# One start address modulo 256 for all pages and slots of a decoder layer on one core

## The chip, the core and the metric

The kernel runs on one core of a Trainium2 chip. A core has TensorE (PE, matrix multiplication), VectorE (DVE), ScalarE (ACT), GpSimd (POOL), and SyncE (SP), which here only issues DMAs. A matmul is two instructions: a load of the weights (the stationary operand, 128 x 128 here) and the MATMUL that streams the moving operand, up to 512 columns, from the on-chip memory SBUF and adds into PSUM. The metric is the device time of one execution in microseconds (us); lower is better.

## The reference

One hybrid decoder layer in fp32 over 1,040 positions (16 meta tokens and 1,024 tokens) of width 1,024:

```python
h = h + 0.5 * rms_norm(swiglu(rms_norm(h, g_ffn1_pre), w_ffn1_in, w_ffn1_out), g_ffn1_post)
u = rms_norm(h, g_mix_pre)
q, k, v, f_logit, c_b, c_c, c_in, gate_a, gate_c = split_cols(u @ w_in)
y_attn = forgetting_attention(q, k, v, log_sigmoid(f_logit + b_forget)) @ w_attn_branch
y_conv = (c_b * short_conv(c_c * c_in, conv_w)) @ w_conv_branch
mixed = (sigmoid(gate_a) * y_attn + sigmoid(gate_c) * y_conv) @ w_out
h = h + rms_norm(mixed, g_mix_post)
h = h + 0.5 * rms_norm(swiglu(rms_norm(h, g_ffn2_pre), w_ffn2_in, w_ffn2_out), g_ffn2_post)
```

The feed-forward width is 2,816 (22 tiles of 128), there are 8 heads of 64, and the meta positions are dropped at the end.

## The kernel before, in words

**Split products.** Each fp32 operand is split into a rounded part h (type fp32r) and a rest l; a product is three matmuls, h·h, h·l and l·h (`mm3`, lines 137 to 141). `split_into` makes the parts: ScalarE casts (L134), VectorE subtracts (L135).

**Seven products.** The feed-forward blocks and their output products each use a scheme of seven half-size products (P1 to P7) in place of eight. In `ffn_in` there are 22 tiles t; each loads its weights on SyncE, splits them into pages, and runs P1, P2, P6, P7, P5, P4, P3. In the first block (names `w...`) the operands of P1, P2, P6 and P4 have rows of W0 = 528 elements and are streamed as two halves of 264 columns; P7, P5 and P3 stream 512. In the second block (names `v...`) all stream 512: 7 products of 12 matmuls. The results go to DRAM (g1d, g2d).

**Output products.** `product_out` (first block, psum names P1 to P7) and `product2` (second block, names 2P1 to 2P7) read g1d or g2d and w_out back, batch by batch of two k tiles; `prep_a` makes the weights side (ahP, alP), `prep_b` the moving side (bhP, blP). For the next products sums are kept in the running buffers RA and RB. `mix_input` normalises the result and makes the mixer's input um0 (meta tokens and the first 512 tokens) and um1 (the last 512), again as h and l, with 4 k tiles in a slot. V's weights wv come right behind, as two pairs: 264 columns wide (half 0, with the forget logits) and 256 wide (half 1).

**Memory.** Four pools stand one behind the other in SBUF. `const` is small and unchanged. `rg` has pages by use: 4 for h, 4 for l, 3 for raw loads r, each of 1,056 elements (4,224 bytes). `zp` has 14 slots z00 to z13 of 2,112 elements (8,448 bytes) for operands of a whole stage. `lp` has ten pages L0 to L9 of 1,056 elements. A page is given again when all that read it is done. In the built program the eight h and l pages begin at 64 and 192 modulo 256 by turns, and so do the pages of `lp`; every slot begins at 192. A row of 528 elements is 2,112 bytes, 64 more than a multiple of 256.

**What sets the order.** A scheduler puts each engine's instructions in one fixed order when the kernel is built, from a timeline that it plans itself and from the priorities in the code (`tc.high_priority` for loads and splits). At run time an engine works off its list and waits where an operand isn't ready; what stands behind waits too. ScalarE also issues DMAs. A change of buffers changes dependencies, and so that order. The first two b tiles of P1 (k0 = 0 and 2, `early`) take pages of `rg`, because they are split while the last tile of the block still runs.

Of the kernel before, what the change touches and what calls it, by code (L numbers as in the profile page):

```python
# [8 lines left out]
F32 = mybir.dt.float32  # L9
F32R = mybir.dt.float32r  # L10
# [3 lines left out]
P = 128  # L14
D = 1024
KT = D // P
META = 16
SEQ = 1024
L = SEQ + META
# [10 lines left out]

H = 512
W0 = H + META


CQ, CK, CV, CCB, CCC, CCI, CGA = 0, 512, 1024, 1544, 2056, 2568, 3080
# [28 lines left out]
def hybrid_layer(ctx, tc, x, meta, w_in, b_forget, conv_w, w_attn, w_conv, w_out,  # L64
# [8 lines left out]
    V, S, G = nc.vector, nc.scalar, nc.gpsimd  # L73
# [10 lines left out]
    pp = ctx.enter_context(tc.tile_pool(name="pp", bufs=1, space=PSUM, reuse_waits="tile"))  # L84

    def page(tag, n, name):
        return rg.tile([P, 1056], F32 if tag == "r" else F32R, tag=tag, bufs=3 if tag == "r" else 4, name=name)[:, :n]

    def slot(i, a, name, dt=F32R):

# [3 lines left out]
    def blk4(i, n, name, dt=F32R):  # L94
        return zp.tile([P, 4 * W0], dt, tag=f"z{i:02d}", name=name)[:, :4 * n].rearrange("p (k n) -> p k n", k=4)

# [3 lines left out]
    class Turns:  # L100
# [8 lines left out]

        def page(self, name, dt=F32):  # L110
            i = self.turn()
            return lp.tile([P, 2 * W0], dt, tag=f"L{i}", name=name)

        def bank(self, name):
            i = self.turn()
# [17 lines left out]
    def split_into(h, l, src, eng=None):  # L133
        S.copy(h, src)  # L134
        (eng or V).tensor_sub(l, src, f32(h))  # L135
# [324 lines left out]

    U, C11, C21, Vt = (blk4(i, W0, nm, F32) for i, nm in ((1, "y01"), (0, "y00"), (2, "y10"), (3, "y11")))

    def running(slots, n, nm):
        ts = [blk4(i, n, f"{nm}{i}", F32) for i in slots]
# [1 line left out]

    runA, runB = running((7, 8, 9), H, "RA"), running((4, 5, 6), W0, "RB")

    def tileA(tag, k, name):
        return page(tag, k * H, name).rearrange("p (k c) -> p k c", k=k)

    def tileB(tag, k, c, name, early=False):
        t = page(tag, k * c, name) if early else loc[tag].page(name, F32 if tag == "r" else F32R)[:, :k * c]
        return t.rearrange("p (k c) -> p k c", k=k)

    def a_src(f, kh, k0, nk):
# [27 lines left out]
    def prep_b(pr, k0, nk):  # L506
        nm = f"{pr}_{k0}"
        c = H if pr in ("P7", "P5", "P3") else W0
        r = slice(META, W0)
        early = pr == "P1" and k0 < 4  # L510
        with tc.high_priority():
            B = lambda kh, hh: b_src(kh, hh, k0, nk)
            tb = lambda tag, n, x: tileB(tag, nk, n, f"b{x}{nm}", early)
            if pr == "P5":
                R = tb("r", H, "r")
                load(R, B(0, 1))
                t = tb("r", W0, "r2")
                load(t, B(0, 0))
                V.tensor_sub(R, R, t[:, :, r])
                h, l = tb("h", c, "h"), tb("l", c, "l")  # L520
                split_into(h, l, R)
                return Split(h, l)
            R = runB(k0, nk)
            if pr == "P7":
                load(R[:, :, r], B(0, 1))
            raw = tb("r", c, "r")
            load(raw, B(*{"P1": (0, 0), "P2": (1, 0), "P3": (1, 1), "P7": (1, 1), "P6": (0, 0), "P4": (1, 0)}[pr]))
            h, l = tb("h", c, "h"), tb("l", c, "l")
            if pr in ("P1", "P2", "P3"):
                split_into(h, l, raw)  # L530
            elif pr == "P7":
                V.tensor_sub(R[:, :, r], raw, R[:, :, r])
                split_into(h, l, R[:, :, r])
            elif pr == "P6":
                V.tensor_add(R[:, :, r], raw[:, :, r], R[:, :, r])
                V.tensor_copy(R[:, :, :META], raw[:, :, :META])
                split_into(h, l, R)
            else:
                V.tensor_sub(R, raw, R)
                split_into(h, l, R)  # L540
        return Split(h, l)
# [3 lines left out]
    def drain(pr, ms, ps):  # L545

        with tc.high_priority():
            if len(ms) == 1:
                m = ms[0]
                for q, p in enumerate(ps):  # L550
                    w = W0 // 2
                    src = p[:, :w]
                    vw = lambda t: t[:, m, q * w:q * w + w]
                    if pr == "P1":
                        S.copy(vw(U), src)
                    elif pr == "P2":
                        V.tensor_add(vw(C11), vw(U), src)
                    elif pr == "P6":
                        V.tensor_add(vw(Vt), vw(Vt), src)
                        V.tensor_add(vw(U), vw(U), src)  # L560
                    else:
                        V.tensor_add(vw(C21), vw(Vt), src)
            else:
                for m, p in zip(ms, ps):
                    vw = lambda t: t[:, m, rr]
                    if pr == "P7":
                        G.tensor_copy(Vt[:, m, :META], U[:, m, :META])
                        V.tensor_add(vw(Vt), vw(U), p)
                    elif pr == "P5":
                        V.tensor_add(vw(Vt), vw(Vt), p)  # L570
                        V.tensor_add(vw(U), vw(U), p)
                    else:
                        V.tensor_add(vw(U), vw(U), p)
# [4 lines left out]
    def product_out(pr, ps=None):  # L578
        ps = ps or banks_out(pr)
        if pr in ("P7", "P5", "P3"):  # L580
            for k0, nk in batches(2):
                a, b = prep_a(pr, k0, nk), prep_b(pr, k0, nk)
                for k in range(nk):
                    for m in range(4):
                        mm3(ps[m // 2][m % 2], a.at(ALLP, k, slice(m * P, m * P + P)), b.at(ALLP, k),
                            start=k0 + k == 0, stop=k0 + k == FH - 1)
            for j in range(2):
                drain(pr, (2 * j, 2 * j + 1), ps[j])
        else:
            w = W0 // 2  # L590
            for k0, nk in batches(2):
                a, b = prep_a(pr, k0, nk), prep_b(pr, k0, nk)
                for k in range(nk):
                    for m in range(4):
                        for q in range(2):
                            mm3(ps[m][q][:, :w], a.at(ALLP, k, slice(m * P, m * P + P)),
                                b.at(ALLP, k, slice(q * w, q * w + w)), start=k0 + k == 0, stop=k0 + k == FH - 1)
            for m in range(4):
                drain(pr, (m,), ps[m])
# [4 lines left out]
    def mix_input(half):  # L604

        if half == 0:
            g = pages2(11, "g1p")
            gain_row(g[:, 0], g1_post, half=True)
            gain_row(g[:, 1], gm_pre)
            grow[0] = g  # L610
        g = grow[0]
        ys = ((C11, C21), (U, Vt))[half]
        hs, ls = ((4, 5), (6, 10)) if half == 0 else ((7, 8), (9, 0))
        h, l = ([blk4(i, W0, f"um{half}{x}{f}") for f, i in enumerate(t)] for x, t in (("h", hs), ("l", ls)))
        um_[half] = (h, l)

        def enter(i):
            o, wd = BLK[i][1], P if i else META
            py = [psR(f"yp{i}_{f}")[:wd] for f in range(2)]
            for f in range(2):  # L620
                for k in range(4):
                    nc.tensor.transpose(py[f][:, k * P:(k + 1) * P], ys[f][:, k, o:o + wd], ident)
            if half == 0:
                w = pages2(12 + i % 2, f"w1_{i}")
                w = [w[:, 0], w[:, 1]]
            else:
                w = [loc[t].page(f"w1{t}{i}")[:, :D] for t in "rh"]
            rows_ = x[(i - 1) * P:i * P, :] if i else meta
            token_block(py, rows_, h1d[(i - 1) * P:i * P, :] if i else None, g[:, 0], w, wd, f"m{i}")
            return w  # L630

        def leave(i, w):
            o, wd = BLK[i][1], P if i else META
            pts = token_cols(g[:, 1], w, psR, wd, f"m{i}")
            for f in range(2):
                split_into(h[f][:, :, o:o + wd], l[f][:, :, o:o + wd], pts[f])

        staggered([i for i in range(9) if BLK[i][0] == half], enter, leave)

    for pr in ("P1", "P2", "P7", "P6", "P4"):  # L640
        product_out(pr)
    psQ, psR = Turns(0, 1, 2, 3).bank2, Turns(4, 5, 6, 7).bank
    ps = banks_out("P5")
    mix_input(0)
# [12 lines left out]
        return t.rearrange("p a n -> p (a n)")[:, :shape[0] * shape[1]].rearrange("p (a n) -> p a n", a=shape[0])  # L657

    wv = {}
    for half, (c0, w) in enumerate(VHALF):  # L660
        for q in range(2):
            src = w_in[512 * q:512 * q + 512, c0:c0 + w].rearrange("(k p) c -> p k c", p=P)
            wv[half, q] = unit([(src, 0)], f"wv{half}_{q}", kt=4, w=w)
    z = const.tile([P, 9, NH], F32, name="z")

    def um(half, k, c0, n):
        h, l = um_[half]
        return Split(h[k // 4][:, k % 4, c0:c0 + n], l[k // 4][:, k % 4, c0:c0 + n])

    def values_in(blk, pvs):  # L670
# [507 lines left out]
```

## Time and profile before

| | us |
|---|---|
| median of 3 runs | 2278.13 (2277.70 to 2285.56) |
| the profiled execution | 2279.55 |
| its span, first to last instruction | 2277.6 |
| TensorE busy | 2150.1 |
| VectorE busy | 1435.8 |
| ScalarE busy | 775.6 |

The mean granted clock of TensorE over the span is 0.974 (1 is 2.4 GHz, 0.5 is 1.2 GHz). Successive matmuls overlap in the pipeline: the duration of one is not its pace. The pace is read from the start of one matmul to the start of the next in the timeline.

### The profile page before, as it was taken

How to read it: one execution, taken by the hardware profiler on the slowest of the kernel's cores; microseconds unless marked ns; L12 is line 12 of the kernel's file. 1: busy time of each engine (PE TensorE's matmuls, PEld its weight loads, DVE VectorE, ACT ScalarE, POOL GpSimd, SP SyncE). 2: the span in 40 equal slices, each digit the busy share in tenths (PEclk: the TensorE clock that was granted, in tenths of full speed). 3: DMA queues.
4: the chain of work that ended last, by engine and by line, in shares of the span. 5: the costliest groups of instructions: out<-in, count | busy, mean ns of one | idle time of the engine just before them, and what ended most of it. 6: DMA issues, size and time to landing. Idle time of an engine off the chain costs nothing.

```text
span 2277.6 us, 30019 instructions
## 1 busy us (share of the span) xinstructions
PE 2150.1 (94%) x11622; PEld 1849.7 (81%) x11622; DVE 1435.8 (63%) x2332; ACT 775.6 (34%) x1269; POOL 100.9 (4%) x194
## 2 busy tenths in 40 slices
PE   5899999999998999999999999899799999999995
PEld 5799999989886998888878787787688888878874
DVE  7866666645969643345554447756776666647785
ACT  5322222223334421134343435334322222224332
POOL 1000000000001100000000001010000000000000
PEclk9899999999998999999999999999899999999998
DMA  3322222266657542343433283843232222278672
GB/s 131 102 84 84 84 84 71 84 243 209 194 164 231 165 145 69 97 115 94 130 105 107 62 229 119 265 138 102 64 112 83 75 78 78 77 261 269 194 263 102
DMA packets 275462, 305.44 MB, mean 134 GB/s; under 512 B 12812, under 2 KB 181848, under 8 KB 275320
## 3 DMA queue, kind: packets, MB, share of 16 engines
q1 hardware_dynamic: 239568, 242.94, 35.4%
q10 hardware_dynamic: 35720, 60.59, 7.7%
q8 instruction: 91, 1.49, 0.3%
q14 instruction: 51, 0.42, 0.1%
q0 software_dynamic: 32, 0.00, 0.0%
HBM read 233.47 MB, written 57.36 MB: 128 GB/s over the span
## 4 chain that ended last, share of the span: by engine, by line
PE 82%; DMA 8%; DVE 6%; issue 2%; ACT 2%; SPq 0%; POOL 0%; ACTq 0%; DVEq 0%; POOLq 0%
PE wP L139 6%; PE wP L140 6%; PE wP L141 6%; PE vP L141 6%; PE vP L140 6%; PE vP L139 6%; PE 2P L140 2%; PE 2P L141 2%; PE 2P L139 2%; PE pg L139 2%; PE pg L141 2%; PE pg L140 2%; PE P L140 2%; PE P L141 2%; PE P L139 2%
## 5 line engine op out<-in xcount | busy, mean ns | idle before, releaser
L139 PE MATMUL P<-bhP,ahP 128*128 128x264 f32 (+1 forms) x484 | 147.8, 323 | 14.5 <-ACT bhP L134 10.3
L140 PE MATMUL P<-blP,ahP 128*128 128x264 f32 (+1 forms) x484 | 157.2, 326 | 4.0 <-DVE ms_m0b L181 3.7
L141 PE MATMUL P<-bhP,alP 128*128 128x264 f32 (+1 forms) x484 | 156.2, 325 | 0.7 <-DVE alP L135 0.7
L140 PE MATMUL 2P<-lb2P,ha2P 128*128 128x512 f32 x308 | 122.5, 398 | 6.1 <-DVE lb2P L135 6.1
L141 PE MATMUL 2P<-hb2P,la2P 128*128 128x512 f32 x308 | 121.8, 396 | 0.0
L139 PE MATMUL 2P<-hb2P,ha2P 128*128 128x512 f32 x308 | 113.7, 396 | 3.8 <-ACT hb2P L134 2.3
L139 PEld LDWEIGHTS P<-bhP,ahP 128*128 128x128 f32 x484 | 91.6, 193 | 22.5 <-ACT bhP L134 11.7
L140 PEld LDWEIGHTS P<-blP,ahP 128*128 128x128 f32 x484 | 95.3, 197 | 11.2 <-DVE ms_m0b L181 4.1
L141 PEld LDWEIGHTS P<-bhP,alP 128*128 128x128 f32 x484 | 95.1, 197 | 7.2 <-DVE alP L135 1.0
L135 DVE TENSOR_TENSOR hbc<-tp,hbc 128x512 fp32r<-128x512 f32 (+1 forms) x112 | 67.2, 610 | 24.3 <-ACT hbc L134 23.5
L134 ACT CAST hbc<-tp 128x512 fp32r<-128x512 f32 (+1 forms) x112 | 56.8, 525 | 62.1 <-PE tp L905 54.8
L140 PEld LDWEIGHTS 2P<-lb2P,ha2P 128*128 128x128 f32 x308 | 58.7, 191 | 20.6 <-DVE lb2P L135 7.4
L139 PEld LDWEIGHTS 2P<-hb2P,ha2P 128*128 128x128 f32 x308 | 57.9, 189 | 18.4 <-ACT hb2P L134 3.5
L141 PEld LDWEIGHTS 2P<-hb2P,la2P 128*128 128x128 f32 x308 | 58.6, 191 | 13.3 <-DVE la2P L135 0.3
L879 PE MATMUL sc<-k,q 128*128 128x392 f32 (+6 forms) x224 | 56.5, 347 | 6.0 <-DMA k<-ha 2.5
L884 ACT ACTIVATE p<-p,mn 128x1040 f32<-128x1040 f32 (+3 forms) x64 | 50.5, 790 | 31.2 <-DVE mn L880 27.3
L139 PE MATMUL wP<-u1T4h,w 128*128 128x264 f32 x176 | 51.4, 292 | 4.5 <-ACT w L134 4.5
L139 PE MATMUL pg<-um0h,g_h 128*128 128x512 f32 x128 | 50.9, 398 | 2.1 <-ACT gt L806 2.1
L139 PE MATMUL pg<-um1h,g_h 128*128 128x512 f32 x128 | 51.6, 403 | 1.2 <-ACT gt L806 0.8
L139 PE MATMUL wP<-u1T2h,ws32h 128*128 128x264 f32 x176 | 50.6, 289 | 1.1 <-ACT u1T2h L134 1.1
L140 PE MATMUL wP<-u1T2l,ws32h 128*128 128x264 f32 x176 | 50.8, 289 | 0.8 <-DVE u1T2l L135 0.8
L141 PE MATMUL pg<-um1h,g_l 128*128 128x512 f32 x128 | 51.1, 400 | 0.0
(769 smaller groups left out, 6720.5 us busy)
## 6 DMA issues: line engine op xcount, KB each, us to landing
arP<-in_w_ffn_out_dram SPq DMA_DIRECT2D x35, 512.0 KB
ra2P<-g2d SPq DMA_DIRECT2D x35, 512.0 KB
rb2P<-in_w_ffn_out_dram SPq DMA_DIRECT2D x35, 512.0 KB
wrb<-in_w_ffn_in_dram SPq DMA_DIRECT2D x22, 512.0 KB
vrb<-in_w_ffn_in_dram SPq DMA_DIRECT2D x22, 512.0 KB
g2d<-vuc ACTq DMA_DIRECT2D x44, 256.0 KB
brP<-g1d SPq DMA_DIRECT2D x20, 528.0 KB
wra<-in_w_ffn_in_dram SPq DMA_DIRECT2D x19, 512.0 KB
```

Of the source, the lines that this page charges most:

```text
L134: S.copy(h, src)
L135: (eng or V).tensor_sub(l, src, f32(h))
L139: mm(o, a.h, b.h, start=start, stop=False)
L140: mm(o, a.h, b.l, start=False, stop=False)
L141: mm(o, a.l, b.h, start=False, stop=stop)
L879: mm(sc[:, :ke - k0], q[:, s, qt * P:qt * P + P], k[:, k0:ke], start=s == 0, stop=s == 1)
L884: S.activation(p[:, :nk], p[:, :nk], AF.Exp, bias=low, scale=-1.0, accum_out=mn[:, 3:4])
```

## The change

Pages and slots get lengths that are multiples of 256 bytes: h and l pages 1,024 elements, r pages and the pages of `lp` 1,088; slots had one already. With that all of them begin at 64 modulo 256. What no longer fits into 1,024 elements moves: the early b tiles of P1 (2 x 528) go to slots z02 and z03 (`begin`), which hold the output accumulators C21 and V only from P7 on; the 264-wide pair of V's weights goes to pages L6 to L9 (`wide`). The slots of um1 get rows of 512 elements without the 16 columns of the meta tokens, so that its k tiles lie 2,048 bytes apart. Lines behind the insertions are 4 to 30 lines further down in the changed kernel.

```diff
+PAGE = 1088
...
     def page(tag, n, name):
-        return rg.tile([P, 1056], F32 if tag == "r" else F32R, tag=tag, bufs=3 if tag == "r" else 4, name=name)[:, :n]
+        w, dt, b = (PAGE, F32, 3) if tag == "r" else (D, F32R, 4)
+        return rg.tile([P, w], dt, tag=tag, bufs=b, name=name)[:, :n]
...
         def page(self, name, dt=F32):
             i = self.turn()
-            return lp.tile([P, 2 * W0], dt, tag=f"L{i}", name=name)
+            return lp.tile([P, PAGE], dt, tag=f"L{i}", name=name)[:, :2 * W0]
...
-    U, C11, C21, Vt = (blk4(i, W0, nm, F32) for i, nm in ((1, "y01"), (0, "y00"), (2, "y10"), (3, "y11")))
+    U, C11 = (blk4(i, W0, nm, F32) for i, nm in ((1, "y01"), (0, "y00")))
+    acc = {}
...
+    begin = {}
+    for tag, i in (("h", 2), ("l", 3)):
+        t = slot(i, 2, f"begin{tag}")
+        for j in range(2):
+            begin[tag, 1 + j] = t[:, j]
...
-    def tileB(tag, k, c, name, early=False):
-        t = page(tag, k * c, name) if early else loc[tag].page(name, F32 if tag == "r" else F32R)[:, :k * c]
+    def tileB(tag, k, c, name, early=0):
+        if early:
+            t = page(tag, k * c, name) if tag == "r" else begin[tag, early][:, :k * c]
+        else:
+            t = loc[tag].page(name, F32 if tag == "r" else F32R)[:, :k * c]
...
-        early = pr == "P1" and k0 < 4
+        early = 1 + k0 // 2 if pr == "P1" and k0 < 4 else 0
...
-        h, l = ([blk4(i, W0, f"um{half}{x}{f}") for f, i in enumerate(t)] for x, t in (("h", hs), ("l", ls)))
+        h, l = ([blk4(i, H if half else W0, f"um{half}{x}{f}") for f, i in enumerate(t)]
+                for x, t in (("h", hs), ("l", ls)))
...
-                split_into(h[f][:, :, o:o + wd], l[f][:, :, o:o + wd], pts[f])
+                c = slice(o - META * half, o - META * half + wd)
+                split_into(h[f][:, :, c], l[f][:, :, c], pts[f])
...
     for pr in ("P1", "P2", "P7", "P6", "P4"):
+        if pr == "P7":
+            acc["V"], acc["C21"] = (blk4(i, W0, nm, F32) for i, nm in ((3, "y11"), (2, "y10")))
         product_out(pr)
+    C21, Vt = acc["C21"], acc["V"]
...
     wv = {}
+    loc = {"r": Turns(0, 1, 2), "h": Turns(3, 5, 4)}
+    wl = Turns(6, 7, 8, 9)
+
+    def wide(tag, n, name):
+        return page(tag, n, name) if tag == "r" else wl.page(name, F32R)[:, :n]
+
     for half, (c0, w) in enumerate(VHALF):
...
-            wv[half, q] = unit([(src, 0)], f"wv{half}_{q}", kt=4, w=w)
+            wv[half, q] = unit([(src, 0)], f"wv{half}_{q}", kt=4, w=w, get=None if half else wide)
...
     def um(half, k, c0, n):
         h, l = um_[half]
+        c0 -= META * half
```

The instructions of each engine are the same in number and kind; the order differs in two places. The first is ScalarE at the head of the first output product. Here wps21 and wuc21 belong to the last tile of the feed-forward block, ahP1_4 is the weights' part h for k tiles 4 and 5, bhP1_4 the moving part, and g1p, w1_1 and w1_0 are loads for `mix_input`. Before:

```order
L336 ACTIVATE wps21_4399<-wps21_4399 128x528
L134 CAST ahP1_2_4662<-arP1_2_4660 128x1024
L187 DMA g1p_6276<-in_g_ffn1_post_dram 128x1024
L134 CAST bhP1_4_4728<-brP1_4_4726 128x1056
L187 DMA g1p_6276<-in_g_mix_pre_dram 128x1024
L357 DMA g1d_72<-wuc21_4476 128x528
L134 CAST bhP1_2_4668<-brP1_2_4666 128x1056
L195 DMA w1_1_6317<-in_x_dram 128x1024
L195 DMA w1_0_6294<-in_meta_tokens_dram 16x1024
L360 ACTIVATE wps21_4399<-wps21_4399 128x512
L362 DMA g1d_72<-wuc21_4476 128x512
L134 CAST ahP1_4_4722<-arP1_4_4720 128x1024
```

And after:

```order
L341 ACTIVATE wps21_4399<-wps21_4399 128x528
L139 CAST ahP1_4_4718<-arP1_4_4716 128x1024
L192 DMA g1p_6274<-in_g_ffn1_post_dram 128x1024
L139 CAST bhP1_4_4724<-brP1_4_4722 128x1056
L192 DMA g1p_6274<-in_g_mix_pre_dram 128x1024
L362 DMA g1d_72<-wuc21_4476 128x528
L139 CAST ahP1_6_4778<-arP1_6_4776 128x1024
L200 DMA w1_1_6315<-in_x_dram 128x1024
L200 DMA w1_0_6292<-in_meta_tokens_dram 16x1024
L365 ACTIVATE wps21_4399<-wps21_4399 128x512
L367 DMA g1d_72<-wuc21_4476 128x512
L139 CAST ahP1_8_4838<-arP1_8_4836 128x1024
```

The casts of ahP1_4 and ahP1_6 stand ahead of the loads w1 and of the second issue to g1d. Right behind, still on ScalarE, before:

```order
L134 CAST ahP1_6_4782<-arP1_6_4780 128x1024
L134 CAST bhP1_10_4908<-brP1_10_4906 128x528
L134 CAST ahP1_8_4842<-arP1_8_4840 128x1024
L134 CAST bhP1_6_4788<-brP1_6_4786 128x1056
L134 CAST ahP1_10_4902<-arP1_10_4900 128x512
L134 CAST ahP2_0_4954<-arP2_0_4952 128x1024
```

And after:

```order
L139 CAST ahP1_8_4838<-arP1_8_4836 128x1024
L139 CAST ahP1_10_4898<-arP1_10_4896 128x512
L139 CAST bhP1_10_4904<-brP1_10_4902 128x528
L139 CAST ahP2_0_4950<-arP2_0_4948 128x1024
L139 CAST bhP1_6_4784<-brP1_6_4782 128x1056
L139 CAST ahP2_2_5010<-arP2_2_5008 128x1024
```

The cast of bhP1_6 still comes behind that of bhP1_10, which waits for a page that P1 reads.

The second place is ScalarE in the middle of P5, where um0h0 and um0h1 are parts of the mixer's input for the meta tokens (block m0) and wv0_0 is the first 264-wide tile of V's weights. Before:

```order
L206 DMA h1d_74<-w1_1_6317 128x1024
L134 CAST bhP5_6_6648<-brP5_6_6643 128x1024
L134 CAST ahP3_0_6762<-RA7_4586 128x1024
L134 CAST um0h0_6280<-m0u0_6338 128x4x16
L134 CAST um0h1_6281<-m0u1_6343 128x4x16
L195 DMA w1_2_6362<-in_x_dram 128x1024
L198 ACTIVATE w1_2_6362,sh_m2_6364<-yp2_0_6352 128x512
L198 ACTIVATE w1_2_6362,sh_m2_6364<-yp2_1_6353 128x512
L212 ACTIVATE w1_1_6317,sh_m1b_6376<-w1_1_6317 128x1024
```

And after:

```order
L211 DMA h1d_74<-w1_1_6315 128x1024
L139 CAST bhP5_6_6646<-brP5_6_6641 128x1024
L139 CAST ahP3_0_6760<-RA7_4584 128x1024
L139 CAST wv0_0_h_6973<-wv0_0_r_6975 128x1056
L139 CAST um0h0_6278<-m0u0_6336 128x4x16
L139 CAST um0h1_6279<-m0u1_6341 128x4x16
L200 DMA w1_2_6360<-in_x_dram 128x1024
L203 ACTIVATE w1_2_6360,sh_m2_6362<-yp2_0_6350 128x512
L203 ACTIVATE w1_2_6360,sh_m2_6362<-yp2_1_6351 128x512
```

The cast of wv0_0 came 38 rows further down; now it stands between ahP3_0 and um0h0.

## Rows read from the trace of the kernel before

**Rows 1.** the page, busy time, share of the span and instructions of each engine
```profile
PE 2150.1 (94%) x11622; PEld 1849.7 (81%) x11622; DVE 1435.8 (63%) x2332; ACT 775.6 (34%) x1269; POOL 100.9 (4%) x194
```

**Rows 2.** by stretch: length, busy time (instructions) by engine, granted clock, DMA share, GB/s
```profile
495.00:541.00 46.00, 38.21 (x268) 36.98 (x268) 16.67 (x16) 13.90 (x19) 3.51 (x2) 0.89 0.71 242
671.00:750.00 79.00, 65.88 (x284) 52.11 (x285) 68.93 (x93) 34.22 (x59) 7.43 (x10) 0.89 0.68 221
975.00:1425.00 450.00, 431.63 (x2298) 364.49 (x2297) 241.74 (x650) 187.56 (x384) 37.79 (x92) 0.98 0.43 119
1640.00:2025.00 385.00, 385.00 (x1660) 312.58 (x1659) 257.74 (x346) 109.39 (x139) 0.00 (x0) 1.00 0.32 95
2044.00:2197.00 153.00, 152.75 (x662) 124.46 (x663) 119.01 (x125) 65.69 (x86) 3.13 (x3) 1.00 0.72 237
```

**Rows 3.** timeline of TensorE, first feed-forward block, tiles 10 and 11: start, duration, instruction
```profile
255.21 0.29 PE L139 MATMUL wP<-u1B11h,wah 128*128 128x264 f32 x1
...
261.05 0.28 PE L139 MATMUL wP<-u1T2h,ws32h 128*128 128x264 f32 x1
...
263.97 0.40 PE L139 MATMUL wP<-u1T3h,ws32h 128*128 128x512 f32 x1
...
266.70 0.40 PE L139 MATMUL wP<-u1T1h,ws14h 128*128 128x512 f32 x1
...
275.20 0.28 PE L139 MATMUL wP<-u1B11h,wah 128*128 128x264 f32 x1
...
281.05 0.29 PE L139 MATMUL wP<-u1T2h,ws32h 128*128 128x264 f32 x1
...
283.99 0.40 PE L139 MATMUL wP<-u1T3h,ws32h 128*128 128x512 f32 x1
...
286.79 0.40 PE L139 MATMUL wP<-u1T1h,ws14h 128*128 128x512 f32 x1
```

**Rows 4.** timeline of TensorE, second feed-forward block, tiles 9 and 10
```profile
1778.01 0.40 PE L139 MATMUL vP<-u2B11h,vah 128*128 128x512 f32 x1
...
1791.98 0.39 PE L139 MATMUL vP<-u2T4h,v 128*128 128x512 f32 x1
...
1794.76 0.40 PE L139 MATMUL vP<-u2B22h,vs14h 128*128 128x512 f32 x1
...
1811.50 0.39 PE L139 MATMUL vP<-u2T4h,v 128*128 128x512 f32 x1
...
1814.22 0.39 PE L139 MATMUL vP<-u2B22h,vs14h 128*128 128x512 f32 x1
...
1817.00 0.40 PE L139 MATMUL vP<-u2B11h,vah 128*128 128x512 f32 x1
```

**Rows 5.** timeline of TensorE, last output product, three block starts
```profile
2074.84 0.40 PE L139 MATMUL 2P<-hb2P,ha2P 128*128 128x512 f32 x1
...
2080.43 0.40 PE L139 MATMUL 2P<-hb2P,ha2P 128*128 128x512 f32 x1
...
2085.92 0.39 PE L139 MATMUL 2P<-hb2P,ha2P 128*128 128x512 f32 x1
```

**Rows 6.** timeline at P1's two waits, TensorE and ScalarE, idle time before in brackets
```profile
511.64 0.39 PE L139 MATMUL P<-bhP,ahP 128*128 128x264 f32 x1 [3.73 <-ACT ahP L134]
...
524.06 0.39 PE L139 MATMUL P<-bhP,ahP 128*128 128x264 f32 x1 [2.68 <-ACT bhP L134]
...
521.45 0.63 ACT L134 CAST bhP<-brP 128x528 fp32r<-128x528 f32 x1 [8.92 <-issue]
```

**Rows 7.** the chain that ended last, from 505 to 525: start, duration, what
```profile
494.38 15.65 DMA RA<-in_w_ffn_out_dram
...
510.11 0.33 ACTq L362
```

**Rows 8.** timeline of the load of V's weights on SyncE and a cast on ScalarE
```profile
700.95 0.37 SPq L147 DMA_DIRECT2D wv_r<-in_w_in_dram  x1
...
705.61 0.20 ACT L134 CAST um0h<-m0u 128x64 fp32r<-128x64 f32 x1
```

More of the change, by code (lines that the diff above doesn't have):

```diff
@@ L553, in drain @@
                     vw = lambda t: t[:, m, q * w:q * w + w]
+                    C21, Vt = acc.get("C21"), acc.get("V")
                     if pr == "P1":
@@ L565, in drain @@
                     vw = lambda t: t[:, m, rr]
+                    Vt = acc["V"]
                     if pr == "P7":
```

## The prediction

> **What bounds the kernel now.** I read the page's busy shares first, then the busy time by stretch, then single matmuls in the timeline, and the waits last. TensorE is busy for 94% of the span, the next engine, VectorE, for 63% [rows 1]. By stretch [rows 2] the second feed-forward block (1640 to 2025) has TensorE busy for 385.00 of 385.00 us at a granted clock of 1.00 (the upper level, 2.4 GHz); its output product (2044 to 2197) for 152.75 of 153; attention and gates (975 to 1425) for 431.63 of 450 at 0.98. In these nothing but the time from one matmul's start to the next can give anything back. Two stretches are different. At the head of the first output product (495 to 541) TensorE is busy for 38.21 of 46 us at 0.89, and from 671 to 750 for 65.88 of 79 us, with VectorE at 68.93: there faster matmuls only wait longer.
>
> So the question is what sets a matmul's pace. Matmuls that follow each other without a wait are not all equally fast, and the difference goes with addresses. In the program before, the eight h and l pages of rg are 4,224 bytes long and so begin at 64 and 192 modulo 256 by turns; so do the ten pages of lp; the fourteen slots of zp (8,448 bytes) all begin at 192. Which page a tile holds is read from the addresses in the built program. I call a matmul aligned when its own weights, its moving operand and the next matmul's weights begin at the same byte modulo 256.
> In the first feed-forward block tile 10's P7 (weights at 192, moving T3 at 192) takes 263.97 to 266.70, 2.73 us for 12 matmuls of 512 columns, 227.5 ns each; tile 11's P7 (weights at 64, the same T3) 283.99 to 286.79, 233.3 ns each [rows 3]. In the second block P4 of tile 9 has its weights at 64: 1791.98 to 1794.76, 231.7 ns; P4 of tile 10 has them at 192 like T4: 1811.50 to 1814.22, 226.7 ns. The two tiles from 1778.01 to 1817.00 average 38.99 us over 168 matmuls, 232.1 ns [rows 4]; P4 of tile 10 is the only aligned product of these fourteen, since h and l pages elsewhere lie at different bytes. In the last output product a block of 24 with its two operands 128 apart takes 5.59 us (232.9 ns) and the next, aligned one 5.49 us (228.8 ns) [rows 5]. With 264 columns there is no such step: P1 and P2 of tile 10 (weights at 64) take 255.21 to 261.05 for 48 matmuls, 121.7 ns, of tile 11 (at 192) 275.20 to 281.05, 121.9 ns [rows 3].
>
> **The change part by part.** No instruction is added or removed; the engines' counts are the same.
>
> Addresses. After the change every page and slot begins at 64 modulo 256, and um1 (rows of 512) starts each of its rows there too. Of 6,200 matmuls with 512 columns some 5,700 are then aligned, before some 1,700. What is left are the projections from um0, whose rows are still 528 and start 16 elements in.
> - Second feed-forward block: 22 tiles of 84 matmuls, 1,848. From 232.1 to 227.5 (the slower of the two aligned values) is 4.6 ns, 8.5 us; with 226.7 it is 10.0; if addresses are not the cause, 0. I take 8.5.
> - First feed-forward block: 792 matmuls with 512 columns, 353 of them aligned already. 439 by 5.8 ns (P7) is 2.5 us; P7 may be the best of the three products, so I take 2.0. Its 264-wide matmuls: 0, at most 0.2 ns by 3,992, 0.8 us either way.
> - Last output product: 924 matmuls, some 523 not aligned now, by 4.2 ns (232.9 less 228.8, rounded up): 2.2 us. The stretch also has the DMA engines at 0.72 [rows 2], so some of it may go into waits.
> - The rest that becomes aligned: 849 projections from um1 (conv, gates, q, k), 308 in the two branch products, 193 in the output projection, 102 in P7 of the first output product, 1,452 together. No row here shows them aligned; the bounds are 0 and 5.4 ns (232.1 less 226.7), 0 to 7.8 us. I take the nearest price, 4.2 ns, 6.1 us, and 70% of it for the path, since these stages also wait for softmax and splits: 4.3 us. P5 and P3 (671 to 750) count nothing: VectorE and DMA set them.
> Here the trace stands against a rule. The Trainium skill (TensorE: Matmul & The Clock Gate, section Step-by-step: what each phase is for) says that the moving operand and the weight load have two independent read ports into SBUF, so that loading the next weights takes nothing from the running matmul. By that rule a relative address can't matter and this part would be 0. Rows 3 to 5 differ from it by 4 to 6 ns a matmul, and the measurement decides.
>
> The head of the first output product. P1 is 264 matmuls of 264 columns, 32.1 us at 121.7 ns. The 46 us from 495 to 541 hold 268, so 13.4 us are lost [rows 2]: waits of 3.73 and 2.68 us on casts of ScalarE [rows 6], and a mean clock of 0.89, which between the levels 1.2 and 2.4 GHz is 10 us at the lower, 5 us lost. The first wait is for the cast of ahP1_4. It stands on ScalarE behind two DMA issues, the second of which (g1d) went out at 510.11 only when a load of RA had landed (issued at 494.38, 15.65 us long) [rows 7]; the cast followed at once, and the matmul at 511.64. The early b tiles now have slots of their own (z02 and z03, free once B21 was last read), so the h and l pages are free for ahP1_4 and ahP1_6, and both casts stand ahead of these issues. The 3.73 us go, and about half of the clock loss, 2.5 us: 6.2 us. What is late next is bhP1_6: its cast still stands behind that of bhP1_10, which waits for P1_4's matmuls to give back page L3 (ScalarE idle for 8.92 us before 521.45 in rows 6), with one more cast between, as before. So the 2.68 us stay, and may become 4 if the g1d issue is held beyond P1_4's end, which is now earlier. I take 5.5; bounds: minus 1 (the moved casts delay the last silu) and 9 (the clock never falls).
>
> V's weights. The 264-wide pair moves from rg to pages 6 to 9 of lp. Their raw loads are where they were on SyncE's queue, but the cast of wv0_0 is now right behind ahP3_0 and ahead of um0h0. In the trace the load is issued at 700.95 and um0h0's cast runs at 705.61 [rows 8]. If it lands 6 us later, ScalarE stands idle for 1 to 2 us and the cast adds 1; behind it are the squares of token block 2, which free the PSUM banks for block 3. In exchange bhP5_8's cast moves ahead of two squares. The second pair's page is given back only by P3's last matmul, but the program now starts with the 256-wide half, which is ready. I take 0, with 3 us either way.
>
> Sum: 8.5 + 2.0 + 2.2 + 4.3 + 5.5 = 22.5 us. The profiled execution took 2279.55 us (a span of 2277.6 and 1.95 around it), which gives 2257.0; it lies 1.4 us above the median of the runs, 2278.13, so I forecast 2255.6 for the median, 2256.
>
> **The rivals.**
> Gains kept only where TensorE is never idle: the two feed-forward blocks, 10.5 us, and 1.5 elsewhere; the rest waits for softmax, DMAs and the stored gates, and at P1 the wait moves from ahP1_4 to bhP1_6 in full. For it: 0.72 DMA share in the last product and the order on ScalarE that is unchanged for bhP1_6. Against it: 96% busy in attention. 2266.
> Addresses are not the cause: the pace goes with which page is being refilled by a split while it is read, and the equal start changes nothing. Then only P1's 5.5 us remain: 2272.6. For it: pages at 64 and at 192 are filled by different transfers. Against it: the same pace at the same addresses in three products of different stages. It is where the skill's two independent ports would lead.
> Slower: ScalarE is held at the cast of wv0_0 in the middle of P5. Everything behind it (um0h0, the squares, bhP5_8) feeds TensorE, which has no other work from 671 to 750. If the load took as long as the 15.65 us of the RA load, it would land at 716.6 and cost 12 us, not enough; it decides from 23 us on (the sum of the gains), a landing after 727, and with 28 us the time is 2284. Against it: it is issued behind few loads.
>
> **How the numbers follow.** Forecast 0.70, at 2256, by itself 2246 to 2263 (all prices at 226.7 or 5.4 ns and 9 for P1 at one end, 228.8 for the second block and 0 for P1 at the other). Gains only where never idle 0.15, at 2266; addresses not the cause 0.11; slower 0.04. About 0.5%, 11 us, is what a measurement of this kernel tells from no change, so faster means below 2266.7: 0.70 and two thirds of 0.15, 0.80. Same: 0.16. Slower: 0.04. The range 2246 to 2268 leaves out the second and third rivals' upper parts and little below.
>
> **What would show it.** The two tiles from 1778 on would take 38.2 us or less for 168 matmuls, with every product near 227 ns and no difference between even and odd tiles; P7 near 227.5 in every tile of the first block; 264-wide matmuls unchanged at 121.7. At the head of P1 one wait of TensorE fewer, and a clock above 0.89. From P5's start to P3's end no change beyond 3 us. The prediction is wrong if the paces stay at 232, or if they fall to 227 and the span doesn't follow.

## The result, and the profile after

The changed kernel takes 2255.93 us (median of 6 runs, 2252.41 to 2261.59), the kernel before 2279.91 us beside it: a ratio of 0.9893, 95% interval 0.9882 to 0.9905, some 24 us. One of the six runs of the kernel before took 2418.31 us; it is a slow run, and the ratio is of fast runs alone. The forecast was 2256, with a range of 2246 to 2268. The profiled execution has a span of 2254.2 us, 23.4 us shorter than that of before, and the mean granted clock over the span is 0.974 in both.

The page's first row, and the busy time by stretch (columns as in [rows 2]; the stretches are those of before, moved to where the work now lies):

```profile
PE 2122.8 (94%) x11622; PEld 1843.3 (82%) x11622; DVE 1434.2 (64%) x2332; ACT 775.1 (34%) x1269; POOL 103.8 (5%) x194
```

```profile
492.00:538.00 46.00, 39.86 (x308) 39.11 (x307) 17.24 (x16) 15.09 (x22) 4.42 (x5) 0.96 0.78 267
...
967.00:1417.00 450.00, 431.33 (x2329) 366.07 (x2327) 245.37 (x658) 189.09 (x387) 37.76 (x92) 0.99 0.43 120
1625.00:2010.00 385.00, 385.00 (x1701) 318.88 (x1700) 263.66 (x354) 112.09 (x142) 3.05 (x1) 1.00 0.34 103
```

TensorE is busy for the same share, 94%, and for 27 us less with the same instructions; VectorE and ScalarE did not get faster (1434.2 and 775.1 us against 1435.8 and 775.6). In the second feed-forward block the same 385 us, busy throughout at full clock, hold 1,701 matmuls instead of 1,660 [rows 2]. That is the signature of a faster pace, not of fewer waits. Attention holds 2,329 matmuls in 450 us instead of 2,298.

The timeline of TensorE in the first feed-forward block, tiles 10 and 11 (start, duration, instruction), which answers to [rows 3]:

```profile
254.72 0.28 PE L144 MATMUL wP<-u1B11h,wah 128*128 128x264 f32 x1
...
260.55 0.28 PE L144 MATMUL wP<-u1T2h,ws32h 128*128 128x264 f32 x1
...
263.46 0.40 PE L144 MATMUL wP<-u1T3h,ws32h 128*128 128x512 f32 x1
...
266.19 0.39 PE L144 MATMUL wP<-u1T1h,ws14h 128*128 128x512 f32 x1
...
283.29 0.40 PE L144 MATMUL wP<-u1T3h,ws32h 128*128 128x512 f32 x1
...
286.02 0.39 PE L144 MATMUL wP<-u1T1h,ws14h 128*128 128x512 f32 x1
```

P7 takes 2.73 us for 12 matmuls, 227.5 ns, in tile 10 and in tile 11, where it had been 2.73 and 2.80. The 48 matmuls of 264 columns in P1 and P2 take 5.83 us, 121.5 ns; they had 121.7. The same view of the second block, tiles 9 and 10, answers to [rows 4]:

```profile
1760.41 0.39 PE L144 MATMUL vP<-u2B11h,vah 128*128 128x512 f32 x1
...
1774.01 0.39 PE L144 MATMUL vP<-u2T4h,v 128*128 128x512 f32 x1
...
1776.73 0.39 PE L144 MATMUL vP<-u2B22h,vs14h 128*128 128x512 f32 x1
...
1793.05 0.39 PE L144 MATMUL vP<-u2T4h,v 128*128 128x512 f32 x1
...
1795.77 0.39 PE L144 MATMUL vP<-u2B22h,vs14h 128*128 128x512 f32 x1
...
1798.49 0.39 PE L144 MATMUL vP<-u2B11h,vah 128*128 128x512 f32 x1
```

The two tiles take 38.08 us for 168 matmuls, 226.7 ns each, where they took 38.99. P4 takes 2.72 us in both; before, 2.78 in the odd tile and 2.72 in the even one.

Where the 23.4 us of the span lie is read from the start of the same matmul in both traces (the first or the last of a stage):

| stage | measured, us | term of the forecast, us |
|---|---|---|
| first feed-forward block, up to P1's first matmul | -2.6 | -2.0 |
| P1 of the first output product | -4.9 | -5.5 |
| P2, P7, P6, P4 | -1.0 | P7 in the rest |
| P5 and P3 | +1.3 | 0, 3 either way |
| V, mixer, attention, branch products, output projection | -6.7 | -4.3 (the rest) |
| second feed-forward block | -9.7 | -8.5 |
| last output product | +0.2 | -2.2 |
| sum | -23.4 | -22.5 |

Two of these need a look. At the head of P1 the timeline of TensorE has these waits (idle time before in brackets); they answer to [rows 6]:

```profile
499.31 0.39 PE L144 MATMUL P<-beginh,ahP 128*128 128x264 f32 x1 [3.24 <-DVE wps L364]
...
516.48 1.24 PE L144 MATMUL P<-bhP,ahP 128*128 128x264 f32 x8 [2.68 <-ACT bhP L139]
```

The wait of 3.73 us on ahP1_4 is gone, that of 2.68 us on bhP1_6 stands there to the last digit, and a wait on the last tile's PSUM has grown to 3.24 us. The mean granted clock of the 46 us rose from 0.89 to 0.96. Between the levels 1.2 and 2.4 GHz a mean of 0.96 is 3.7 us at the lower one, where 0.89 was 10.

In the last output product the four products 2P2, 2P5, 2P6 and 2P3 win 0.45 to 0.54 us each (29.92 against 30.37 to 30.46), 2.04 us together. Behind 2P7 it is given back: from the first matmul of 2P7 to the first of 2P4 it is 38.54 us, where it was 35.36. The first batch of 2P4 needs a load; VectorE and TensorE in the timeline of the changed kernel, where the MATMUL is 2P4's first:

```profile
2196.40 1.22 DVE L1121 TENSOR_TENSOR RB<-rb2P,RB 128x1024 f32<-128x1024 f32 x1 [4.53 <-DMA rb2P<-in_w_ffn_out_dram]
2198.81 1.65 PE L144 MATMUL 2P<-hb2P,ha2P 128*128 128x512 f32 x3 [3.71 <-ACT hb2P L139]
```

The same VectorE instruction in the kernel before:

```profile
2218.32 1.23 DVE L1091 TENSOR_TENSOR RB<-rb2P,RB 128x1024 f32<-128x1024 f32 x1 [1.19 <-DMA rb2P<-in_w_ffn_out_dram]
```

VectorE waits 4.53 us instead of 1.19 for that load, and TensorE behind it 3.71 us instead of 1.26.

### The profile page after: what moved, and what is told of

Its sections match the earlier page's. It is cut to its first block, busy times and chain, and to the rows that moved or that the text cites. A ratio compares the mean times of both kernels' runs of the same rounds, so it can differ in the third digit from the quotient of the medians.

```text
span 2254.2 us, 30020 instructions
## 1 busy us (share of the span) xinstructions
PE 2122.8 (94%) x11622; PEld 1843.3 (82%) x11622; DVE 1434.2 (64%) x2332; ACT 775.1 (34%) x1269; POOL 103.8 (5%) x194
## 4 chain that ended last, share of the span: by engine, by line
PE 78%; DMA 9%; DVE 8%; ACT 2%; issue 2%; SPq 1%; POOL 0%; ACTq 0%; DVEq 0%; POOLq 0%
PE wP L144 6%; PE wP L145 6%; PE wP L146 6%; PE vP L144 6%; PE vP L145 6%; PE vP L146 6%; PE pg L144 2%; PE pg L145 2%; PE pg L146 2%; PE 2P L145 2%; PE 2P L146 2%; PE P L145 2%; PE 2P L144 2%; PE P L146 2%; PE P L144 2%
## 5 line engine op out<-in xcount | busy, mean ns | idle before, releaser
L145 PE MATMUL P<-blP,ahP 128*128 128x264 f32 (+1 forms) x452 | 146.4, 326 | 4.1 <-DVE ms_m0b L186 2.8
L144 PE MATMUL P<-bhP,ahP 128*128 128x264 f32 (+1 forms) x452 | 136.3, 320 | 9.7 <-ACT bhP L139 6.8
L146 PE MATMUL P<-bhP,alP 128*128 128x264 f32 (+1 forms) x452 | 145.3, 324 | 0.0
L144 PEld LDWEIGHTS P<-bhP,ahP 128*128 128x128 f32 x452 | 84.3, 191 | 16.4 <-ACT bhP L139 7.8
L145 PEld LDWEIGHTS P<-blP,ahP 128*128 128x128 f32 x452 | 87.8, 194 | 11.7 <-DVE blP L140 6.0
L146 PEld LDWEIGHTS P<-bhP,alP 128*128 128x128 f32 x452 | 87.6, 194 | 5.6
L145 PE MATMUL wP<-u1T4l,w 128*128 128x264 f32 x176 | 51.1, 290 | 0.0
```

The costliest lines, as they stand in the source:

```text
L144: mm(o, a.h, b.h, start=start, stop=False)
L145: mm(o, a.h, b.l, start=False, stop=False)
L146: mm(o, a.l, b.h, start=False, stop=stop)
```

## The experiments

A matmul is called unaligned here unless its own weights and the next matmul's weights both begin at the byte of its moving operand modulo 256; the counts are of matmuls with 512 columns, from the addresses in the built programs. Before: 4,519 (6,200 less the 1,681 aligned ones); after: 476. Each ratio is to runs of the kernel before that were taken beside the kernel of its row, so it need not be the quotient of two medians of the table. In the built programs every engine of lengths, shift128, shift32, start128, um1rows and moves has the order of the changed kernel; only addresses differ.

| kernel | unaligned | median, us | ratio to before | 95% interval | second block, ns per matmul without wait |
|---|---|---|---|---|---|
| before | 4,519 | 2279.91 | 1 | | 232.2 |
| after | 476 | 2255.93 | 0.9893 | 0.9882 to 0.9905 | 226.8 |
| lengths | 3,682 | 2274.55 | 0.9970 | 0.9956 to 0.9985 | 230.1 |
| shift128 | 5,589 | 2279.92 | 1.0008 | 0.9997 to 1.0018 | 232.3 |
| shift32 | 5,722 | 2283.48 | 1.0010 | 1.0000 to 1.0020 | 232.4 |
| start128 | 476 | 2255.80 | 0.9891 | 0.9876 to 0.9906 | 226.8 |
| um1rows | 1,121 | 2260.62 | 0.9914 | 0.9890 to 0.9938 | 226.7 |
| beginonly | 3,905 | 2278.35 | 0.9995 | 0.9986 to 1.0005 | 230.1 |
| moves | 3,905 | 2275.26 | 0.9983 | 0.9972 to 0.9994 | 230.1 |

**lengths: the starts undone alone.**

```diff
-PAGE = 1088
+PAGE = 1056
...
-        w, dt, b = (PAGE, F32, 3) if tag == "r" else (D, F32R, 4)
+        w, dt, b = (PAGE, F32, 3) if tag == "r" else (PAGE, F32R, 4)
```

> The changed kernel with the page lengths of before (1,056 elements): every engine has the order of the changed kernel, the moved tiles and the shorter rows of um1 stay, only the starts differ. Unaligned 512-column matmuls: 3,682, against 476 in the changed kernel and 4,519 before. Theory (the distance modulo 256 between weights and moving operand sets the pace): the changed kernel won 23.4 us, of which 5.0 at the head of P1; the other 18.4 for 4,043 matmuls less is 4.55 ns each, so 3,206 more cost 14.6 us: 2270.5, with the tiles of the second feed-forward block alternating between 227 and 231 to 234 ns again, and the head of P1 as fast as after the change. Rival (moved tiles and order give the gain, the start does not): 2256, and 227 ns in every tile.

Measured 2274.55 us, 0.9970 of before. The rival's 2256 is out. The difference to the changed kernel is 0.0077 of 2280, 17.6 us for 3,206 matmuls, 5.5 ns each, more than the 4.55 reckoned. Timeline of TensorE, P4 of tiles 9 and 10 of the second block:

```profile
1783.16 0.39 PE L144 MATMUL vP<-u2T4h,v 128*128 128x512 f32 x1
...
1785.96 0.39 PE L144 MATMUL vP<-u2B22h,vs14h 128*128 128x512 f32 x1
...
1802.51 0.39 PE L144 MATMUL vP<-u2T4h,v 128*128 128x512 f32 x1
...
1805.23 0.39 PE L144 MATMUL vP<-u2B22h,vs14h 128*128 128x512 f32 x1
```

2.80 us (233 ns) in tile 9 and 2.72 (226.7 ns) in tile 10: the alternation is back, with nothing changed but addresses. P1 takes 40.1 us, as fast as after the change (40.6; before 45.5), so that gain belongs to the moves.

**shift128: all pages of a kind at one byte, but weights and operand 128 apart.**

```diff
-        w, dt, b = (PAGE, F32, 3) if tag == "r" else (D, F32R, 4)
+        w, dt, b = (2 * W0, F32, 3) if tag == "r" else (D, F32R, 4)
```

> The changed kernel with raw pages of 1,056 elements: the same order on every engine, and all slots and pages behind the raw ones begin 128 bytes later (at 192 modulo 256), while the h and l pages in front of them stay at 64. All pages of one kind begin at the same byte, but weights and moving operands lie 128 apart almost everywhere (5,589 unaligned matmuls against 476). Theory (distance between weights and moving operand): 5,113 by 4.55 ns, 23.3 us more, 2279; the second feed-forward block at 231.7 ns in every tile, as the tiles before with both weights pages at 64 and the operand at 192. Rival 1 (what counts is that the pages alternate, that is, that two weights pages in turn begin at different bytes): 2256 and 227 ns. Rival 2 (order and moves): 2256.

Measured 2279.92 us, the theory's number; both rivals fall. The whole gain is gone though no page alternates and the order is that of the changed kernel. P4 and the product behind it, P3, in tiles 9 and 10:

```profile
1788.65 0.40 PE L144 MATMUL vP<-u2T4h,v 128*128 128x512 f32 x1
...
1791.42 0.40 PE L144 MATMUL vP<-u2B22h,vs14h 128*128 128x512 f32 x1
...
1794.21 0.39 PE L144 MATMUL vP<-u2B11h,vah 128*128 128x512 f32 x1
...
1808.17 0.40 PE L144 MATMUL vP<-u2T4h,v 128*128 128x512 f32 x1
...
1810.94 0.40 PE L144 MATMUL vP<-u2B22h,vs14h 128*128 128x512 f32 x1
...
1813.73 0.39 PE L144 MATMUL vP<-u2B11h,vah 128*128 128x512 f32 x1
```

P3, with weights at 64 and its operand at 192, takes 2.79 us, 232.5 ns, in both tiles: no alternation, and the slow pace throughout. So it is the distance between the streams that costs, not the turn of the pages. P4 is another matter. Its weights lie in pages of `lp`, which also moved to 192, so it is aligned, and still it takes 2.77 us, 231 ns, in both tiles. Its twelve steps in tile 9 are 235, 233, 236, 224, 231, 236, 228, 233, 231, 226, 227 and 232 ns (the last one into P3): behind an unaligned product the pace comes down to 227 only near the end. So distance 0 alone does not make every matmul fast. That this kernel is no slower than before in spite of 1,070 more unaligned matmuls fits P1, which takes 38.1 us in it.

**shift32: a distance of 32 bytes.**

```diff
-        w, dt, b = (PAGE, F32, 3) if tag == "r" else (D, F32R, 4)
+        w, dt, b = (PAGE - 24, F32, 3) if tag == "r" else (D, F32R, 4)
```

> The changed kernel with raw pages of 1,064 elements: slots and all pages behind the raw ones begin at 32 modulo 256, h and l pages stay at 64, every engine keeps its order. 5,722 matmuls are unaligned, by 32 bytes instead of 128. In the group of single matmuls 32 bytes cost as much as 128 (233.3 against 232.3 ns). Theory (any distance but 0 costs some 5 to 6 ns): as with the 128-byte shift, 2279 to 2283, the second feed-forward block at 232 to 233 ns. Rival (half of 256 is the bad distance, a small one is harmless): 2256 to 2262.

Measured 2283.48 us, as the theory said: 32 bytes cost as much as 128. By the ratios, 0.0117 of 2280, 26.7 us for 5,246 matmuls, is 5.1 ns each; shift128 gives the same 5.1 (26.2 us for 5,113). These sums hold P1 too, which takes 42.3 us here, 38.1 in shift128 and 40.6 in the changed kernel. P4 and P3 of tile 9:

```profile
1796.00 0.39 PE L144 MATMUL vP<-u2T4h,v 128*128 128x512 f32 x1
...
1798.73 0.39 PE L144 MATMUL vP<-u2B22h,vs14h 128*128 128x512 f32 x1
...
1801.52 0.40 PE L144 MATMUL vP<-u2B11h,vah 128*128 128x512 f32 x1
```

P3, 32 bytes apart, takes 2.79 us (232.5 ns). P4, aligned as in shift128, takes 2.73 (227.5): here the two products side by side show what the distance costs. Why P4 settles at once here and not in shift128 no run shows.

**start128: all starts moved together.**

```diff
-    rows = const.tile([P, P], F32, name="rows")
+    rows = const.tile([P, P + 16], F32, name="rows")[:, :P]
```

> The changed kernel with 64 bytes more in the small constants: every page and slot begins at 128 modulo 256 instead of 64, all distances as in the changed kernel, the same order on every engine. Theory: 2256, 226.8 ns in the second feed-forward block. Rival (64 is a good start in itself): over 2260.

Measured 2255.80 us. Whether all start at 64 or at 128 is worth nothing, as long as the distances stay.

**um1rows: the shorter rows undone.**

```diff
-        h, l = ([blk4(i, H if half else W0, f"um{half}{x}{f}") ...
+        h, l = ([blk4(i, W0, f"um{half}{x}{f}") ...
...
-                c = slice(o - META * half, o - META * half + wd)
+                c = slice(o, o + wd)
...
-        c0 -= META * half
```

> The changed kernel with rows of 528 elements in um1 again (the pages stay at 64). Unaligned matmuls: 1,121 against 476, all in the projections of the mixer. Theory: 645 by 4.55 ns, 2.9 us more, 2258.9, with the projections from um1 near 231 ns. Rival (these stages wait for softmax and splits, so their pace does not reach the end): 2256, whatever the pace.

Measured 2260.62 us (4 runs); its interval overlaps that of the changed kernel, so the sum alone does not decide. The trace does: the second block starts 2.8 us later than in the changed kernel, against 2.9 expected. (P3 had ended 0.8 us earlier, so the stages between lost 3.6.) The mean step of the projections (matmuls with 512 columns and no wait before the next, ns):

| | before | after | um1rows |
|---|---|---|---|
| gates from um0 | 231.6 | 232.0 | 232.1 |
| gates from um1 | 231.8 | 228.9 | 232.1 |
| conv in (pi) from um1 | 232.5 | 226.7 | 231.7 |
| conv b (pb) from um0 | 231.7 | 232.6 | 231.7 |
| conv b (pb) from um1 | 231.9 | 227.1 | 231.7 |

The gates of um0 and um1 use the same weights side by side in the program; um0, whose rows stayed at 528, did not get faster.

**beginonly and moves: the moves without the starts.** The first puts only the early b tiles of P1 into z02 and z03 of the kernel before; the second also puts V's wide pair into pages L6 to L9.

```diff
-        t = page(tag, k * c, name) if early else ...
+        if early:
+            t = page(tag, k * c, name) if tag == "r" else begin[tag, early][:, :k * c]
...
-        early = pr == "P1" and k0 < 4
+        early = 1 + k0 // 2 if pr == "P1" and k0 < 4 else 0
```

> The kernel before with one part of the change: the early b tiles of P1 in slots z02 and z03; page lengths, um1 and V's weights as before. The turn of the pages shifts, so 3,905 matmuls are unaligned against 4,519. Theory: the head of P1 falls from 45.5 us to about 40.5 us as in the changed kernel (5.0 us), the pages that turn give 614 by 4.55 ns, 2.8 us: 7.8 us faster than before in sum, 2270.3 to 2272. Rival (P1's gain comes from the faster matmuls ahead of it, that is, from another meeting of loads and products): the head of P1 stays at 45 us and only the 2.8 us remain, 2275 to 2277.

> The kernel before with the two moves of the change (early b tiles in z02 and z03, V's wide weights in pages 6 to 9 of lp), with the page lengths and um1 rows of before: 3,905 unaligned matmuls, as with the first move alone. Theory: the move of V's weights keeps the 5 us of P1 from being lost at P3, where the first move alone waited 4.5 us more: P3 at 31.5 us, 2275 to 2276. Rival 1 (the wait at P3 comes from P1 ending earlier, whatever holds V's weights): P3 at 36 us, 2278 to 2279. Rival 2 (moves and order alone do what the change does): 2256.

P1 takes 40.7 us in beginonly and 41.7 in moves: the move of the early tiles alone makes P1's gain. The rival of beginonly, P1 at 45 us, falls. But the theory's sum falls too: 0.9995 of before, an interval that holds no change, since the gain did not reach the end. TensorE in its timeline:

```profile
724.30 0.50 PE L139 MATMUL P<-bhP,ahP 128*128 128x512 f32 x1 [1.68 <-DVE y L583]
728.79 1.22 PE L139 MATMUL P<-bhP,ahP 128*128 128x512 f32 x2 [2.83 <-ACT bhP L134]
```

Both are among P3's first matmuls. Its chain of waits shows what the cast waited for:

```profile
719.77 7.90 DMA brP<-g1d
727.70 1.05 ACT bhP L134
```

P3 takes 36.7 us there and 31.4 in moves (before 31.8; P3's own matmuls, without the transposes of the token blocks between them), so with the second move the loss is gone, and moves comes out at 2275.26, as expected. Of its 0.0017 of 2280, 3.9 us, some 3.1 are the 614 matmuls that turning pages made aligned (at 5.1 ns); the moves by themselves are worth little more than nothing at the end. What moves lacks against the changed kernel, with the same order on every engine, is addresses alone: 0.0090 of 2280, 20.5 us of the 24. What in V's weights keeps that load of P3 early was not tried.

**micro: the pace by itself.** The kernel is a list of groups of 96 matmuls, each group with weights at one distance from the moving operand, or with two in turn. It was run once, and so was micro2.

```diff
+    ("d0x", (0,), (0,), 512),
+    ("d128x", (128,), (0,), 512),
...
+    nc.tensor.matmul(ps[:, :cols], w[:, a:a + P], m[:, b:b + cols], start=i == 0, stop=i == 11)
```

> Leaves out the whole layer: 27 groups of 96 matmuls of 128 x 128 fp32r weights that follow each other without a wait and without any write to SBUF beside them; a group sets the distance in bytes from the moving operand to the weights modulo 256 (0, 16, 32, 64 to 224, 256), the common start (0, 64, 128, 192), two weights or two operands in turn, and the columns (512, 384, 264, 256). Theory (distance modulo 256): 226.7 to 228 ns at distance 0 and 256 whatever the start, 231 to 234 at 128, at 264 columns no difference (121.7). Where two weights alternate, the steps of single matmuls tell whether the matmul's own weights or the next weights count; by the case before, both. Rival 1 (a page that is being refilled slows its readers): 227 ns in every group, since nothing is written. Rival 2 (the start modulo 256 itself counts and not the distance): groups with a common start at 64 and 192 differ from 0.

Timeline of TensorE, a row for each group (d and its bytes are the distance, b64 a distance of 0 at the common start 64, c264 and c384 the columns); from one start to the next is 96 steps. Starts count from those of the two tiles, which both lie at 128 modulo 256 in the built program:

```profile
30.12 21.92 PE L74 MATMUL d0x<-m,w 128*128 128x512 f32 x96
51.88 21.93 PE L74 MATMUL d16x<-m,w 128*128 128x512 f32 x96
73.64 22.55 PE L74 MATMUL d32x<-m,w 128*128 128x512 f32 x96
...
140.91 22.47 PE L74 MATMUL d128x<-m,w 128*128 128x512 f32 x96
...
185.62 22.15 PE L74 MATMUL d192x<-m,w 128*128 128x512 f32 x96
207.61 22.56 PE L74 MATMUL d224x<-m,w 128*128 128x512 f32 x96
230.00 21.92 PE L74 MATMUL d256x<-m,w 128*128 128x512 f32 x96
251.76 21.96 PE L74 MATMUL b64x<-m,w 128*128 128x512 f32 x96
...
406.30 11.68 PE L74 MATMUL c264d0x<-m,w 128*128 128x264 f32 x96
...
429.34 11.69 PE L74 MATMUL c264d128x<-m,w 128*128 128x264 f32 x96
```

At distance 0: 21.76 us, 226.7 ns. At 128: 22.31 us, 232.4 ns; 32, 64, 96, 160 and 224 give 233 to 234, 192 only 229, and 256 is 226.7 again. Common starts of 64, 128 and 192 give 227.1: their first twelve steps take 230.2, later ones 226.7 as at 0. Nothing writes to SBUF beside these matmuls, so the refilled page falls, and so does the start as such. With 264 columns the distance changes nothing: 11.68 us a group at 0, 11.69 at 128. Which weights count, the matmul's own or the next ones? Either. In the group with weights at 0, 0 and 128 in turn a step takes 227.0 ns where both are at distance 0, 232.2 where only the next ones are apart and 234.3 where only its own are. The kernel before shows the same, by its trace and the addresses in its program (steps of 512-column matmuls under 260 ns): 228.5 with both at distance 0 (1,594 steps), 232.6 with only the next weights 128 apart (952), 233.1 with only its own (931), 232.9 with both (1,667).

The Trainium skill (TensorE: Matmul & The Clock Gate, section Step-by-step: what each phase is for) gives TensorE two independent read ports and says that "Loading the next tile's weights doesn't steal SBUF read bandwidth from the running matmul." These groups hold only weight loads and the matmuls themselves, and 5.7 ns of 512 columns hang on where the two read. By the rule the time would have been 2272.6, the forecast's second rival. What in the memory makes the difference no run here shows.

**micro2: columns and small shifts.** The same with other groups.

> Leaves out the whole layer: groups of 96 matmuls without waits, as before, now by columns (512 down to 256, at distance 0 and 128), by small shifts of the weights (4 to 28 bytes) and of the moving operand (4 to 240 bytes), and with a weights tile that changes its start every matmul. Theory: starts count in steps of 32 bytes, so shifts of the weights below 32 cost nothing; the cost falls with the columns and is gone at 264, which is why no 264-wide product gained. Rival 1 (cost for a fixed number of stolen accesses per weight load): the same 5 ns at each number of columns. Rival 2 (modulo 16 and not 32): 28 costs as much as 32.

```profile
29.66 21.93 PE L82 MATMUL c512d0x<-m,w 128*128 128x512 f32 x96
51.43 22.48 PE L82 MATMUL c512d128x<-m,w 128*128 128x512 f32 x96
73.75 20.98 PE L82 MATMUL c480d0x<-m,w 128*128 128x480 f32 x96
94.56 21.28 PE L82 MATMUL c480d128x<-m,w 128*128 128x480 f32 x96
...
154.71 18.08 PE L82 MATMUL c416d0x<-m,w 128*128 128x416 f32 x96
172.63 18.09 PE L82 MATMUL c416d128x<-m,w 128*128 128x416 f32 x96
...
343.11 22.56 PE L82 MATMUL w16x<-m,w 128*128 128x512 f32 x96
...
610.59 22.24 PE L82 MATMUL wm16x<-m,w 128*128 128x512 f32 x96
632.67 21.96 PE L82 MATMUL wm16off32x<-m,w 128*128 128x512 f32 x96
```

The distance of 128 costs 5.7 ns at 512 columns (232.4 less 226.7), 3.2 at 480, 1.4 at 448 and none at 416 and 320; 384 has 2.6 again, 264 here 2.0 (121.4 and 123.4; nothing in micro) and 256 even -1.2. The rival of a fixed price falls; the fall is not even. Moving the operand in place of the weights gives what the distance says: by 32, 64, 128, 192 and 224 bytes 233.3, 229.0, 232.3, 233.4 and 233.2 ns, as the weights at 224, 192, 128, 64 and 32. The part on small shifts failed: weights moved by 4, 8, 16 and 28 bytes gave 231 to 233 ns, though 16 bytes in micro had given 226.7, and an operand at 240 (again a distance of 16) gave 226.8. With the operand 16 bytes behind, the theory fails outright: 230.0 ns at distance 0 (wm16x), and 227.1 at distance 32 (wm16off32x, weights at 48). So the distance sets the pace where both starts are multiples of 32 bytes; what holds between them stays open.

## Why the prediction was right

**The pace goes with the distance of the addresses.** Right for starts at multiples of 32 bytes, which all of the kernels' 512-column operands have, and shown from four sides: undone alone (lengths), kept regular but apart (shift128, shift32), moved together (start128), and by itself (micro). The exceptions are P4 of shift128, aligned and slow, and the groups at 16 bytes. The measured price of some 5 ns a matmul is within the 4 to 6 ns that [rows 3 to 5] gave.

**Second feed-forward block, 8.5 us.** Measured 9.7. I took 227.5, the slower of two aligned values; the block's products run at 226.7 to 227.1, and the bound of 10.0 was nearly the value.

**First block, 2.0 us.** Measured 2.6, and the 264-wide matmuls moved by 0.2 ns ([rows 3]: 121.7), inside the bound given for them. But [rows 3] could not show that the distance costs nothing there: with rows of 2,112 bytes, halved, the operands of P1 and P2 begin at eight different bytes modulo 256 in either tile. That comes from micro: 120.0 ns at 0, 32 and 128.

**The rest, 4.3 us.** With P7 (0.6) it measured 7.4, and the factor of 70% hides two opposite errors. The pace of the projections from um1 fell by 3 to 6 ns, and q and k lost 1.6 us of waits as well, 2.2 us in all; but the gates' waits grew by 1.0 us and ate their gain (185.1 us from start to start against 185.0). The output projection won 1.4 us, the conv projections 1.3, and the scores and transposes of attention 1.2, for which no term stood. Why q and k and these last won it was not tried.

**P1, 5.5 us.** The sum was right (4.9) and its working only in part. The 3.73 us went, the 2.68 us stayed, as said; the clock gave more than the 2.5 us I counted (6.4 us less at the lower level, 3.2 us), and a wait I had not named, 3.24 us on the last tile's PSUM, took most of the removed one back. VectorE's subtraction for the last tile (L364) stands behind the split of a b tile, whose cast on ScalarE waited for RB to land; the timeline of both engines:

```profile
496.30 1.07 ACT L139 CAST bhP<-brP 128x1056 fp32r<-128x1056 f32 x1 [10.36 <-DMA RB<-g1d]
497.40 1.26 DVE L140 TENSOR_TENSOR blP<-brP,bhP 128x1056 fp32r<-128x1056 f32 x1 [6.12 <-ACT bhP L139]
498.58 0.68 DVE L364 TENSOR_TENSOR wps<-wps,wP 128x512 f32<-128x512 f32 x1
```

The cast started at 496.30 and the subtraction at 498.58, and TensorE went on at 499.31. That the moved tiles make this gain, and not faster matmuls ahead of them, is shown by lengths and beginonly.

**V's weights, nothing.** P5 and P3 lost 1.3 us, inside the 3 us either way. The rival of a cast of wv0_0 that holds ScalarE did not come.

**Last output product, 2.2 us.** Here the forecast failed: the pace fell as said, 2.04 us in four products, and the start of 2P4, waiting for a load, gave it back. The doubt stood in the text (the stretch has the DMA engines at 0.72), but not the number. The terms were too small by 1.2, 0.6 and 3.1 us (and 0.3 in P2, P6 and P4, which had none), too large by 2.4, 1.3 and 0.6; that leaves 0.9. That the errors cancel, and so 2255.93 meets 2256 so closely, is luck.

## What to carry to other kernels

On a TensorE that is never idle, look up at which byte modulo 256 the weights and the moving operands of 512-column matmuls begin, and make the pitch of every page and row a multiple of 256 bytes; here, with fp32r and new weights for every matmul, that was worth some 2% of each such matmul and 20 us in sum. It is the distance that counts, not the common start, so one odd page length in a pool shifts all that lies behind it. Read the pace from starts of consecutive matmuls, and expect the gain to reach the end only where no load or split is due.

## What the runs showed of the hardware that was not expected

- The step from 416 to 512 columns: no cost of the distance at 416, 5.7 ns at 512, and 2.6 ns at 384 between two widths (416 and 320) without any.
- Weights that change their start every two matmuls can slow the aligned ones too: in the group with starts 0, 0, 128, 128 the steps with own and next weights at distance 0 took 231.2 ns, against 226.7 where all have one start, and P4 of shift128 took 231 behind an unaligned product. It is not always so: 227.0 with starts 0, 0, 128, and 227.5 for P4 of shift32.
- Distance 0 at a common start of 16 took 230.0 ns, at starts of 0, 64, 128 and 192 226.7 to 227.1; with the operand at 16 a distance of 32 took only 227.1.
